# A feed-forward layer and its background tables: state-space table products moved from GpSimd to VectorE

## Chip, core and metric

The kernel runs on one core of a Trainium2 chip. The metric is device time in microseconds, from start to end of one execution. TensorE makes the matrix products, VectorE, ScalarE and GpSimd the elementwise work; SyncE's, ScalarE's and GpSimd's queues start the DMAs.

## What is computed

Eight layers over 512 tokens of 1024 features, in float32: a pooling mixer, a feed-forward layer with a convolution, windowed attention, a second feed-forward layer, an S5 state-space mixer, an MLP, a Mamba-2 mixer and an MLP. The change touches only what S5 needs ahead of time, out of its parameters alone. Cut to that, the reference says

```python
lam_bar = jnp.exp(lam * dt)
b_bar = ((lam_bar - 1) / lam)[..., None] * lax.complex(b_re, b_im)
bu = jnp.einsum('btgh,gph->btgp', u_blk, b_bar)
_, hs = lax.associative_scan(_s5_combine, (a_elems, bu), axis=1)
y = jnp.einsum('btgp,ghp->btgh', hs, c_mat).real
```

with 64 groups of 64 complex states and 16 channels. The kernel takes the tokens in 64 chunks of 8. Inside a chunk everything is products with small matrices: the powers of lam_bar from 0 to 8 (`pr`, `pi`), times B and C. From chunk to chunk the state is turned by a unit phasor and scaled. The tables that this needs (per group: the turns of 64 chunks, the matrices `vp` turned, `c4` and the products `kt`) are written to memory as `d_tab` and `d_k`, and the second feed-forward layer's background and S5 read them later.

## The kernel before

**Tables as background.** `s5_tables` (L535) is a generator: each `yield` ends a step, and other layers call for so many steps (`bg[0](n)`, `work(n)`) between their own work. Its first step is all of `s5_powers` (L558): exponentials and sines on VectorE and ScalarE, then powers one after the other and the repeated squares `step` by complex products on GpSimd (`cmul`, L617 to L623, each six instructions of 128x64). Then come eight rounds of four steps. `s5_phasors` (L645) makes the turns of eight groups by six doublings on GpSimd (L657 to L663, 8 to 256 elements wide), 36 instructions and a scaling, and starts two DMAs to `d_tab` from GpSimd's queue. `s5_mats` (L667) makes the matrices: one step of small VectorE work (L701 to L713: C turned and signed, `b0` and `b1`, of which `b1` has one buffer), then two halves of six 128x512 products each on GpSimd (L725 to L730). After the second half's products the first half's matrices are stored: `s5_store` (L737) transposes `vp` (L748) and multiplies (L749) on TensorE, copies out on ScalarE (L744, L751, L753), adds on VectorE (L757) and starts DMAs from ScalarE's queue. There are 34 steps.

**The layer around it.** Step 1 is taken in the pooling mixer (L916), the others in the body of the first feed-forward layer, `ffn_layer(0, ...)` at L1943. The head makes output tiles 0 and 1. The body (L980) has three phases, tiles 0 to 8, 8 to 16 and 16 to 22. In each phase pairs of tiles are made by products "upward" (96 of 512 columns for a pair: two tiles, gate and value, 8 k tiles, three products each), with four PSUM banks for the four outputs (`psm`, all four in use); VectorE takes them out (`scaled`, L936), convolves (L942, L943) and multiplies (L950), and ScalarE and VectorE part the result into `hi` and `lo` (L326, L328). After the first two phases `project` makes the eight outputs "downward" and `down` (L969) sums them. The third phase's downward products are the tail, made by halves of the tokens behind the body. A pair is followed by 3 steps of the tables, a downward output by 1, and 3 stand ahead of the first pair. `late` makes the rotary table of attention (`rope_tables`, L1024) ahead of the last phase. What is left of the tables is run at the body's end (`end_tables`, L1925). The second feed-forward layer is the same code with other work in its steps: it streams the conditioning's weights, with its sums on VectorE, ScalarE and TensorE (`ada_units`).

**Weights.** SyncE's queue loads chunks of 512 KB into three staging tiles; ScalarE (L204) and VectorE (L205) part each into `wh` and `wl`, of which there are four; a chunk serves 24 products.

**Order and room.** The tile framework fixes each engine's order of instructions when the program is built, by priority (the order of the program, seams raised) on a simulated time line; on the chip every engine runs its list in order. Tiles are slots of pools: `ap` has 31 of 128x512 and holds `hi`, `lo`, the eight outputs `ft`, the tables' `s5v` (2) and `s5buf` (6), the rotary table (2) and, in the last phase, 8 tiles of tail weights; `tp` has 14 for what lives shortly. An instruction that writes a tile waits until the last user of the slot's earlier tile is done.

Of the kernel before, what the change touches and what calls it, by code (L numbers as in the profile page):

```python
# [21 lines left out]
P = 128  # L22
# [7 lines left out]
# order of queueing: how many tiles each stage of a chain over the tiles stays behind the first, the tiles whose part  # L30
# falls to GpSimd, and the projections' steps between the blocks of attention and the chunks of SSD
# [32 lines left out]
def net_kernel(ctx: ExitStack, tc: tile.TileContext, I: dict, out: bass.AP, parts=ALL):  # L64
# [33 lines left out]
    # ---- constants  # L98
# [18 lines left out]
    r = 0  # L117
# [43 lines left out]
    # ---- x, feature-major  # L161
# [48 lines left out]
    def chunks(W, k0, nk, c0, ncol=256, kmax=4, gain=None, **kw):  # L210
        """(hi, lo, first k, k tiles) for the rows of k tiles k0.. and columns c0.. of W."""
        for k in range(0, nk, kmax):
            n = min(kmax, nk - k)
            r = (k0 + k) * P
            yield wchunk(W[r:r + n * P, c0:c0 + ncol].rearrange("(k p) n -> p k n", p=P),
                         gain=gain and (gain[0], gain[1] + k), **kw) + (k, n)
# [14 lines left out]
    def project(W, k0, nk, c0, tiles, xh, xl, evac, **kw):  # L231
        """Output tiles (an even run of them) over all tokens; evac(n, psum, span)."""
# [8 lines left out]
    class Held:  # L241
        """Output tiles taken over one half of the tokens, then over the other; their weights stay for both.
        runs: (W, k0, nk, c0, apart, kwargs) of one or two tiles each, which share a bank; the weights of the last
        `apart` k tiles lie among the activations."""
# [20 lines left out]
        def run(self, hf, xh, xl, evac):  # L265
            """evac(run, tile of the run, psum, span)"""
# [10 lines left out]
    # ---- root mean square over features (partitions and tiles)  # L277
    class Norm:
# [19 lines left out]
        def rs(self, span, eps, out=None):  # L298
            """1/rms of each token of the span, on all partitions."""
# [30 lines left out]
    class Line:  # L330
        """Keeps the instructions given to it in their order on their engine."""
# [11 lines left out]
    def staged(stages, lags):  # L343
        """Takes each k tile through the stages, every stage some tiles behind the first."""
# [13 lines left out]
    def warm_sqrt(after):  # L358
        """Has the square root's table loaded behind the given instruction, ahead of its use."""
# [4 lines left out]
    def behind(instructions):  # L364
        """Queues what it holds behind the given instructions on their engines."""
# [5 lines left out]
    class PreNorm:  # L371
        """The normalized, scaled (and shifted) x, in parts; one span at a time."""
# [40 lines left out]
    class PreScale(PreNorm):  # L413
        """x times the norm's gains alone, in parts; what the products give is then to be scaled by 1/rms."""
# [7 lines left out]
        def parts(self, span):  # L422
            """The two stages that make tile k's parts of the new x."""
# [14 lines left out]
    def post_add(ft, sq, gname, g0, span, nxt, pre):  # L438
        """x += rms_norm(f) over the span; nxt gathers the new squares."""
# [18 lines left out]
    def reduce_angle(a, k):  # L458
        """a less its nearest multiple of two pi; k is scratch."""
# [5 lines left out]
    def exp_exact(x, scr):  # L465
        """x to its exponential, to float32's accuracy; scr(dtype) gives scratch of x's shape."""
# [13 lines left out]
    # ---- a vector times a weight, laid out with features on partitions: in float32 by rows, summed over the  # L480
    # partitions as three bfloat16 parts, which hold all of its bits
    def vecmat(pool, W, ncb, col, done):
        """Steps, to be run between other work; done(cb, sums) takes the features of four tiles."""
# [35 lines left out]
    def ada_units(pool, i):  # L519
        """The modulation silu(c) @ W + b of layer i, and what S5's products make of its shift."""  # L520
# [14 lines left out]
    def s5_tables(pool, dr):  # L535
        """Chunk matrices of the state space, from its parameters alone; steps as of ada_units."""
# [3 lines left out]
        step = []  # L540
        s5_powers(pool, dr, pr, pi, cr, ci, sg, step)
# [5 lines left out]
        buf = [at("s5buf") for _ in range(6)]  # L547
        mats = s5_mats(pool, dr, pr, pi, vr, vi, cr, ci, sg, buf[3:])
        next(mats)
        for n in range(8):  # L550
            s5_phasors(dr, n, step, sg, buf)
            yield
            for _ in range(3):
                next(mats)
                yield
        yield from mats

    def s5_powers(pool, dr, pr, pi, cr, ci, sg, step):  # L558
# [58 lines left out]
        def cmul(orr, oi, ar, ai, br, bi, tmp):  # L617
            G.tensor_tensor(orr, ar, br, ALU.mult)
            G.tensor_tensor(tmp, ai, bi, ALU.mult)
            G.tensor_tensor(orr, orr, tmp, ALU.subtract)  # L620
            G.tensor_tensor(oi, ar, bi, ALU.mult)
            G.tensor_tensor(tmp, ai, br, ALU.mult)
            G.tensor_tensor(oi, oi, tmp, ALU.add)  # L623

        for t in range(2, 9):
            cmul(pr[:, t], pi[:, t], pr[:, t - 1], pi[:, t - 1], pr[:, 1], pi[:, 1], t1)
        # unit phasors of one chunk and its decay
# [3 lines left out]
        e1r, e1i = sm("e1r"), sm("e1i")  # L631
        V.tensor_scalar(e1r, cm, 1.0, None, ALU.add)
        V.tensor_copy(e1i, sn)
# [1404 lines left out]
```

## Time and profile before

| | us |
|---|---|
| runs of the kernel | 2565.32, 2565.53, 2560.61 |
| their median | 2565.32 |
| span of the profiled execution | 2564.4 |
| TensorE busy in it | 2368.0 (92%) |
| VectorE busy | 1687.6 (66%) |
| ScalarE busy | 1148.0 (45%) |
| GpSimd busy | 736.4 (29%) |

The time of the profiled execution itself is not listed apart from these runs; its span, from the first to the last instruction, is the number beside them. Busy shares are means over eight unlike layers, so a stage has to be read by its own stretch of the trace, and an engine with a small share can still be the one that a stage waits for. In the rows PE is TensorE's matmuls, DVE VectorE, ACT ScalarE, POOL GpSimd, SP SyncE; L205 is line 205 of the kernel.

### The profile page before, as it was taken

Reading aid. Unit: us, or ns where it says so; the run is one execution under the profiler, and the core shown is the slowest. Engines: PE = TensorE matmul, PEld = TensorE weight load, DVE = VectorE, ACT = ScalarE, POOL = GpSimd, SP = SyncE. Lnnn points to the kernel's source line nnn. Section 1 sums busy time; section 2 is a strip of 40 time slices with the busy share of each in tenths; the row PEclk is TensorE's granted clock in tenths of the full one; section 3 lists DMA queues with packets and bytes.
Section 4 is the critical chain, followed back from the end, with each engine's and each line's share of the span. In section 5 each row is a group of like instructions: output and inputs, shape, how many; then the busy total and the mean of one; then the engine's idle time right before and its main releaser. Section 6 shows DMA issues by size and latency. Waiting matters only on the chain.

```text
span 2564.4 us, 34249 instructions
## 1 busy us (share of the span) xinstructions
PE 2368.0 (92%) x12485; PEld 1989.4 (78%) x12485; DVE 1687.6 (66%) x2739; ACT 1148.0 (45%) x2054; POOL 736.4 (29%) x1111
## 2 busy tenths in 40 slices
PE   6888996998988999996989899999999999999998
PEld 6756674887677888776878787789887888888888
DVE  6874574667857868687653667665778788633333
ACT  6533342447666544343543433334556454423332
POOL 3989988031212000004120201112043332301110
PEclk8988997999999999998989999999999999999999
DMA  4234333222155555652852255553233332233322
GB/s 121 69 98 114 118 121 101 90 80 66 33 155 158 172 181 164 197 164 76 280 180 91 82 171 185 184 172 95 88 113 106 105 98 95 84 98 99 99 86 71
DMA packets 296761, 311.34 MB, mean 121 GB/s; under 512 B 53569, under 2 KB 251025, under 8 KB 295569
## 3 DMA queue, kind: packets, MB, share of 16 engines
q1 hardware_dynamic: 267729, 274.03, 35.2%
q10 hardware_dynamic: 23680, 17.31, 2.2%
q0 software_dynamic: 5184, 17.83, 2.1%
q8 instruction: 98, 1.61, 0.3%
q14 instruction: 70, 0.57, 0.1%
HBM read 284.92 MB, written 24.18 MB: 121 GB/s over the span
## 4 chain that ended last, share of the span: by engine, by line
PE 63%; DVE 12%; POOL 9%; DMA 6%; issue 5%; ACT 4%; SPq 0%; DVEq 0%; ACTq 0%; POOLq 0%
PE mm L220 18%; PE mm L219 18%; PE mm L221 18%; DVE wl L205 3%; DMA as<-in_ada_w 3%; POOL s5buf L659 1%; ACT wh L204 1%; PE pb L1710 1%; DVE u L400 1%; PE mm L1640 1%; PE mm L1641 1%; PE mm L1642 1%; DVE lo L328 1%; PE pn L306 1%; DVE u L450 1%
## 5 line engine op out<-in xcount | busy, mean ns | idle before, releaser
L220 PE MATMUL mm<-h,wh 128*128 128x512 f32 (+1 forms) x1792 | 669.4, 374 | 26.5 <-DVE h L428 13.2
L219 PE MATMUL mm<-h,wh 128*128 128x512 f32 (+1 forms) x1792 | 665.9, 374 | 27.2 <-ACT h L401 11.4
L221 PE MATMUL mm<-h,wl 128*128 128x512 f32 (+1 forms) x1792 | 666.3, 372 | 1.9 <-DVE wl L205 1.9
L205 DVE TENSOR_TENSOR wl<-ws,wh 128x1024 fp32r<-128x1024 f32 (+1 forms) x367 | 499.5, 1365 | 252.2 <-ACT wh L204 239.4
L204 ACT ACTIVATE wh<-ws 128x1024 fp32r<-128x1024 f32 (+1 forms) x367 | 387.2, 1059 | 531.0 <-PE mm L220 435.8
L220 PEld LDWEIGHTS mm<-h,wh 128*128 128x128 f32 x1792 | 348.1, 194 | 86.4 <-DVE h L428 16.9
L219 PEld LDWEIGHTS mm<-h,wh 128*128 128x128 f32 x1792 | 348.1, 195 | 84.1 <-ACT h L401 12.6
L219 PE MATMUL mm<-hi,wh 128*128 128x512 f32 (+1 forms) x1056 | 372.7, 357 | 27.4 <-ACT hi L326 22.3
L221 PEld LDWEIGHTS mm<-h,wl 128*128 128x128 f32 x1792 | 348.7, 195 | 56.8 <-DVE wl L205 2.3
L220 PE MATMUL mm<-lo,wh 128*128 128x512 f32 (+1 forms) x1056 | 373.4, 355 | 11.8 <-DVE lo L328 11.8
L221 PE MATMUL mm<-hi,wl 128*128 128x512 f32 (+1 forms) x1056 | 373.1, 355 | 0.0
L219 PEld LDWEIGHTS mm<-hi,wh 128*128 128x128 f32 x1056 | 201.1, 191 | 55.9 <-ACT hi L326 23.9
L1264 POOL TENSOR_TENSOR r<-r 128x512 f32<-128x512 f32 x64 | 88.0, 1379 | 517.3 <-ACT r L1260 384.2
L220 PEld LDWEIGHTS mm<-lo,wh 128*128 128x128 f32 x1056 | 202.1, 191 | 40.1 <-DVE lo L328 14.2
L221 PEld LDWEIGHTS mm<-hi,wl 128*128 128x128 f32 x1056 | 202.3, 192 | 26.5
L504 DVE SCALAR_TENSOR_TENSOR aa<-as,cond,aa 128x512 f32<-128x512 f32 x168 | 130.1, 774 | 112.8 <-DMA as<-in_ada_w 111.5
L296 POOL TENSOR_TENSOR acc<-acc,sq 128x256 f32<-128x256 f32 (+1 forms) x64 | 62.1, 972 | 389.6 <-ACT sq L295 377.7
L328 DVE TENSOR_TENSOR lo<-r,hi 128x512 fp32r<-128x512 f32 x64 | 48.1, 756 | 76.4 <-ACT hi L326 76.2
L1285 DVE SCALAR_TENSOR_TENSOR x<-mm,mod,x 128x512 f32<-128x512 f32 (+1 forms) x76 | 48.9, 662 | 60.3 <-PE mm L221 60.3
L512 ACT ACTIVATE ab<-aa 128x512 bf16<-128x512 f32 x72 | 45.0, 625 | 90.6 <-DVE aa L504 50.5
L1319 POOL DMA_DIRECT2D vt<-d_tab x16 | 8.8, 555 | 264.7 <-PE mm L221 260.8
L326 ACT ACTIVATE hi<-r 128x512 fp32r<-128x512 f32 x64 | 40.2, 630 | 70.4 <-POOL r L1264 70.3
(494 smaller groups left out, 4084.5 us busy)
## 6 DMA issues: line engine op xcount, KB each, us to landing
ws<-in_mlp_w SPq DMA_DIRECT2D x124, 512.0 KB, 3.9
as<-in_ada_w SPq DMA_DIRECT2D x192, 256.0 KB, 3.1
ws<-in_ffn_w_in SPq DMA_DIRECT2D x88, 512.0 KB, 4.2
ws<-in_m_w_in SPq DMA_DIRECT2D x41, 512.0 KB, 3.7
ws<-in_ffn_w_out SPq DMA_DIRECT2D x40, 512.0 KB, 4.7
ws<-in_w_o SPq DMA_DIRECT2D x16, 512.0 KB, 3.5
ct<-d_tab SPq DMA_DIRECT2D x8, 1024.0 KB, 5.9
ws<-in_s_w_glu SPq DMA_DIRECT2D x16, 512.0 KB, 5.8
```

The lines of the kernel that those rows point to most:

```text
L204: A.activation(h_, s_, AF.Copy)
L205: V.tensor_tensor(l_, s_, f(h_), ALU.subtract)
L219: T.matmul(ps, wh, xh, start=first, stop=False)
L220: T.matmul(ps, wh, xl, start=False, stop=False)
L221: return T.matmul(ps, wl, xh, start=False, stop=last).ins
L296: eng.tensor_tensor(dst, dst, sq[:, a:b], ALU.add)
L326: hi_ = A.activation(hi[:, ts], src, AF.Copy)
L328: return hi_, V.tensor_tensor(lo[:, ts], src, f(hi[:, ts]), ALU.subtract)
L504: V.scalar_tensor_tensor(acc, st, col(k), acc, ALU.mult, ALU.add)
L512: A.activation(parts[j], acc, AF.Copy)
L1264: G.tensor_tensor(r, r, r, ALU.mult)
L1285: V.scalar_tensor_tensor(xT[n][:, ts], ps, md(i, 5, n), xT[n][:, ts], ALU.mult, ALU.add)
```

## The change

The powers are made by doubling, three complex products of 64, 128 and 256 elements in place of seven of 64. The turns of a group's 64 chunks become an outer product of two tables of eight (`near`: turns 0 to 7, `far`: turns 0, 8, ... 56), six instructions of 512 elements for eight groups in place of 37 of 8 to 512. All of these products go from GpSimd to VectorE, and GpSimd keeps two memsets for each table of eight and `dd` in the store. The copy into `cp` goes to ScalarE. The turns' DMAs go from GpSimd's queue to SyncE's. `vp` and its scratch are tiles of their own in place of parts of `s5buf`. A half's products are two steps, and its matrices are stored after the next half's, so with one half waiting longer than before. There are 63 steps in place of 34, the powers being five of them, and the first feed-forward layer takes 4 at a time in place of 3, so that 61 are taken by the end of its body. The rotary table's frequencies are filled by 32 memsets in place of 128.

```diff
@@ s5_tables @@
     def s5_tables(pool, dr):
         pr, pi = (pool.tile([P, 9, 64], F32, name=nm("s5k")) for _ in range(2))
         cr, ci = (pool.tile([P, 64], F32, name=nm("s5k")) for _ in range(2))
         sg = pool.tile([P, 1], F32, name="s5sg")
-        step = []
-        s5_powers(pool, dr, pr, pi, cr, ci, sg, step)
+        far, near = ([at("s5ph").rearrange("p (g t) -> p g t", t=8) for _ in range(2)] for _ in range(2))
+        yield from s5_powers(pool, dr, pr, pi, cr, ci, sg, far, near)
         yield
         vr, vi = (at("s5v").rearrange("p (t g) -> p t g", t=8) for _ in range(2))
         for s in range(8):
             A.activation(vr[:, s], pr[:, 7 - s], AF.Copy)
             A.activation(vi[:, s], pi[:, 7 - s], AF.Copy, scale=sg)
-        buf = [at("s5buf") for _ in range(6)]
-        mats = s5_mats(pool, dr, pr, pi, vr, vi, cr, ci, sg, buf[3:])
+        mats = s5_mats(pool, dr, pr, pi, vr, vi, cr, ci, sg)
         next(mats)
         for n in range(8):
-            s5_phasors(dr, n, step, sg, buf)
-            yield
-            for _ in range(3):
+            yield from s5_phasors(dr, n, far, near)
+            for _ in range(5):
                 next(mats)
                 yield
         yield from mats
 
-    def s5_powers(pool, dr, pr, pi, cr, ci, sg, step):
+    def s5_powers(pool, dr, pr, pi, cr, ci, sg, far, near):
@@ s5_powers, s5_phasors @@
         def cmul(orr, oi, ar, ai, br, bi, tmp):
-            G.tensor_tensor(orr, ar, br, ALU.mult)
...
-        for t in range(2, 9):
-            cmul(pr[:, t], pi[:, t], pr[:, t - 1], pi[:, t - 1], pr[:, 1], pi[:, 1], t1)
+            V.tensor_tensor(orr, ar, br, ALU.mult)
...
+        yield
+        for w in (1, 2, 4):
+            o = slice(w + 1, 2 * w + 1)
+            top = [a[:, w].unsqueeze(1).broadcast_to([P, w, 64]) for a in (pr, pi)]
+            tmp = tt("cm")[:, :64 * w].rearrange("p (t g) -> p t g", t=w)
+            cmul(pr[:, o], pi[:, o], pr[:, 1:w + 1], pi[:, 1:w + 1], *top, tmp)
         r8 = dr["r8"]
         V.tensor_scalar(r8, ea, 8.0, None, ALU.mult)
         exp_exact(r8, scr())
-        e1r, e1i = sm("e1r"), sm("e1i")
-        V.tensor_scalar(e1r, cm, 1.0, None, ALU.add)
-        V.tensor_copy(e1i, sn)
-        e2r, e2i = sm("e2r"), sm("e2i")
+        yield
+        er_, ei_ = sm("e1r"), sm("e1i")
+        V.tensor_scalar(er_, cm, 1.0, None, ALU.add)
+        V.tensor_scalar(ei_, sn, sg, None, ALU.mult)
+        turn = er_, ei_
+        free = iter([(sm("e2r"), sm("e2i")), (lr, li), (dt, th), (er, nr), (ni, sc), (er_, ei_), (cm, sn), (ea, t1)])
+        def squared(z):
+            o, t = next(free), tt("cm")[:, :64]
+            V.tensor_tensor(o[0], z[0], z[0], ALU.mult)
+            V.tensor_tensor(t, z[1], z[1], ALU.mult)
+            V.tensor_tensor(o[0], o[0], t, ALU.subtract)
+            V.scalar_tensor_tensor(o[1], z[0], 2.0, z[1], ALU.mult, ALU.mult)
+            return o
         for _ in range(3):
-            cmul(e2r, e2i, e1r, e1i, e1r, e1i, t1)
-            e1r, e1i, e2r, e2i = e2r, e2i, e1r, e1i
-        free = [e2r, e2i, lr, li, dt, th, er, nr, ni, sc]
...
-    def s5_phasors(dr, n, step, sg, buf):
+            turn = squared(turn)
+        for tab in (near, far):
+            G.memset(tab[0][:, :, 0:1], 1.0)
+            G.memset(tab[1][:, :, 0:1], 0.0)
+            for w in (1, 2, 4):
+                by = [a.unsqueeze(2).broadcast_to([P, 64, w]) for a in turn]
+                tmp = tt("cm")[:, :64 * w].rearrange("p (g t) -> p g t", t=w)
+                lo, up = slice(0, w), slice(w, 2 * w)
+                cmul(tab[0][:, :, up], tab[1][:, :, up], tab[0][:, :, lo], tab[1][:, :, lo], *by, tmp)
+                if tab is near or w < 4:
+                    turn = squared(turn)
+            yield
+    def s5_phasors(dr, n, far, near):
         g8 = slice(8 * n, 8 * n + 8)
-        ct, si = (b.rearrange("p (g c) -> p g c", g=8) for b in buf[:2])
...
-        for j in range(6):
-            w = 1 << j
...
-        nc.gpsimd.dma_start(dr["tab"][n][:, :512], ct.rearrange("p g c -> p (g c)"))
-        nc.gpsimd.dma_start(dr["tab"][n][:, 512:1024], si.rearrange("p g c -> p (g c)"))
-    def s5_mats(pool, dr, pr, pi, vr, vi, cr, ci, sg, buf):
+        wide = lambda t: t.rearrange("p (g a b) -> p g a b", g=8, a=8)
+        fr, fi = (t[:, g8].unsqueeze(3).broadcast_to([P, 8, 8, 8]) for t in far)
+        nr_, ni_ = (t[:, g8].unsqueeze(2).broadcast_to([P, 8, 8, 8]) for t in near)
+        for i, (a, b, c, d, op) in enumerate(((fr, nr_, fi, ni_, ALU.subtract), (fr, ni_, fi, nr_, ALU.add))):
+            o, t = tt("ph"), tt("ph")
+            V.tensor_tensor(wide(o), a, b, ALU.mult)
+            V.tensor_tensor(wide(t), c, d, ALU.mult)
+            V.tensor_tensor(o, o, t, op)
+            nc.sync.dma_start(dr["tab"][n][:, 512 * i:512 * i + 512], o)
+            yield
+    def s5_mats(pool, dr, pr, pi, vr, vi, cr, ci, sg):
@@ s5_mats @@
             for hf in range(2):
                 g4 = slice(8 * gb + 4 * hf, 8 * gb + 4 * hf + 4)
                 o4 = slice(4 * hf, 4 * hf + 4)
-                vp, tc_ = (b.rearrange("p (g t h) -> p g t h", g=4, t=8) for b in (buf[1 + hf], buf[0]))
+                wide = lambda t: t.rearrange("p (g t h) -> p g t h", g=4, t=8)
                 cp = pool.tile([P, 4, 9, 16], F32, tag="cp", bufs=2, name=nm("cp"))
                 tp8 = lambda a: a.unsqueeze(2).broadcast_to([P, 4, 8, 16])
                 pw = lambda a: a[:, :, g4].rearrange("p t g -> p g t").unsqueeze(3).broadcast_to([P, 4, 8, 16])
-                G.tensor_copy(cp[:, :, 0], cc[:, 0, o4])
-                G.tensor_tensor(cp[:, :, 1:], tp8(cc[:, 0, o4]), pw(pr[:, 1:]), ALU.mult)
-                G.tensor_tensor(tc_, tp8(cc[:, 1, o4]), pw(pi[:, 1:]), ALU.mult)
-                G.tensor_tensor(cp[:, :, 1:], cp[:, :, 1:], tc_, ALU.add)
-                G.tensor_tensor(vp, tp8(b0[:, o4]), pw(vr), ALU.mult)
-                G.tensor_tensor(tc_, tp8(b1[:, o4]), pw(vi), ALU.mult)
-                G.tensor_tensor(vp, vp, tc_, ALU.add)
-                if pend:
-                    s5_store(pool, dr, *pend.pop())
+                t = wide(tt("ct"))
+                A.activation(cp[:, :, 0], cc[:, 0, o4], AF.Copy)
+                V.tensor_tensor(cp[:, :, 1:], tp8(cc[:, 0, o4]), pw(pr[:, 1:]), ALU.mult)
+                V.tensor_tensor(t, tp8(cc[:, 1, o4]), pw(pi[:, 1:]), ALU.mult)
+                V.tensor_tensor(cp[:, :, 1:], cp[:, :, 1:], t, ALU.add)
+                yield
+                vp, t = wide(at("vp")), wide(tt("ct"))
+                V.tensor_tensor(vp, tp8(b0[:, o4]), pw(vr), ALU.mult)
+                V.tensor_tensor(t, tp8(b1[:, o4]), pw(vi), ALU.mult)
+                V.tensor_tensor(vp, vp, t, ALU.add)
                 pend.append((gb, hf, cp, vp, b0, dg))
                 yield
-        s5_store(pool, dr, *pend.pop())
+                if len(pend) > 1:
+                    s5_store(pool, dr, *pend.pop(0))
+        while pend:
+            s5_store(pool, dr, *pend.pop(0))
+            yield
@@ ffn_layer @@
-    def ffn_layer(l, phases, late=None):
+    def ffn_layer(l, phases, late=None, rate=3):
...
-            bg[0](3)
+            bg[0](rate)
...
-                    bg[0](3)
+                    bg[0](rate)
@@ rope_tables @@
         fr = tt("fr")[:1, :P]
         for i in range(32):
-            for r in range(4):
-                G.memset(fr[:, 32 * r + i:32 * r + i + 1], float(ROPE_FREQ[i]))
+            G.memset(fr.rearrange("o (r i) -> o r i", r=4)[:, :, i:i + 1], float(ROPE_FREQ[i]))
@@ net_kernel @@
             layer = ffn_layer(0, ((0, 8), (8, 16), (16, 22)),
-                              lambda: rope_c.update(rope_tables()) if "attn" in names else None)
+                              lambda: rope_c.update(rope_tables()) if "attn" in names else None, 4)
```

## Rows read from the trace of the kernel before

**Rows 1.** Page, 40 slices: busy tenths of POOL, TensorE's granted clock in tenths

```profile
POOL 3989988031212000004120201112043332301110
...
PEclk8988997999999999998989999999999999999999
```

**Rows 2.** Stretches: us, busy (instructions) of PE, PEld, DVE, ACT, POOL, clock, DMA

```profile
101.40:518.30 416.90, 361.01 (x1558) 277.34 (x1557) 271.35 (x326) 162.64 (x222) 317.21 (x624) 0.92 0.37 112
818.00:1131.00 313.00, 311.85 (x1479) 253.62 (x1477) 251.78 (x368) 140.09 (x185) 1.14 (x2) 1.00 0.55 169
...
818.00:892.00 74.00, 74.00 (x343) 60.99 (x341) 67.34 (x98) 42.35 (x55) 0.00 (x0) 1.00 0.53 164
...
450.00:518.30 68.30, 68.30 (x303) 56.27 (x302) 48.34 (x68) 32.04 (x40) 0.70 (x2) 1.00 0.33 101
```

**Rows 3.** TensorE's waits, 101.4 to 518.3: total us, times, longest

```profile
PE mm L219 <- ACT hi L326: 22.3, 3, 11.6
PE pb L748 <- POOL s5buf L730: 19.9, 5, 8.2
PE mm L220 <- DVE lo L328: 10.3, 1, 10.3
PE mm L219 <- DVE u L936: 3.3, 1, 3.3
```

**Rows 4.** VectorE's waits, same stretch

```profile
DVE b L711 <- POOL s5buf L729: 48.3, 6, 15.0
...
DVE lo L328 <- POOL s5buf L728: 12.8, 1, 12.8
```

**Rows 5.** Timeline, VectorE: start us, us, engine, line, operation, out<-in [idle before]

```profile
154.22 14.32 DVE L205 TENSOR_TENSOR wl<-ws,wh 128x1024 fp32r<-128x1024 f32 x1 [2.38 <-ACT wh L204]
...
259.47 11.29 DVE L205 TENSOR_TENSOR wl<-ws,wh 128x1024 fp32r<-128x1024 f32 x1 [3.24 <-ACT wh L204]
...
342.08 7.18 DVE L943 SCALAR_TENSOR_TENSOR tg<-u,vec,tg 128x510 f32<-128x510 f32 x1
...
403.89 12.11 DVE L328 TENSOR_TENSOR lo<-tv,hi 128x512 fp32r<-128x512 f32 x1 [12.84 <-POOL s5buf L728]
```

**Rows 6.** Timeline, GpSimd, beside the first of these

```profile
154.28 1.28 POOL L730 TENSOR_TENSOR s5buf<-s5buf,s5buf 128x512 f32<-128x512 f32 x1
...
167.49 1.60 POOL L663 TENSOR_SCALAR s5buf<-s5buf,s5sg 128x512 f32<-128x512 f32 x1
```

**Rows 7.** Timeline, TensorE: the first and last of 18 like products, and a store

```profile
142.25 0.39 PE L219 MATMUL mm<-h,wh 128*128 128x512 f32 x1
...
153.83 0.39 PE L219 MATMUL mm<-h,wh 128*128 128x512 f32 x1
...
231.60 0.27 PE L748 MATMUL pb<-ident,s5buf 128*128 128x128 f32 x1
...
233.87 0.50 PE L219 MATMUL mm<-hi,wh 128*128 128x512 f32 x1
```

**Rows 8.** Timeline, VectorE, second feed-forward layer

```profile
852.10 0.68 DVE L950 TENSOR_TENSOR tv<-tv,tg 128x512 f32<-128x512 f32 x1
852.70 1.21 DVE L205 TENSOR_TENSOR wl<-ws,wh 128x1024 fp32r<-128x1024 f32 x1
853.84 0.68 DVE L514 TENSOR_TENSOR aa<-aa,ab 128x512 f32<-128x512 f32 x1
```

**Rows 9.** Timeline, VectorE, ahead of the body

```profile
69.36 0.21 DVE L610 TENSOR_TENSOR s5k<-s5k,sc 128x64 f32<-128x64 f32 x1
69.49 0.21 DVE L612 TENSOR_TENSOR t<-nr,lamT 128x64 f32<-128x64 f32 x1
...
69.96 0.28 DVE L708 TENSOR_TENSOR b<-bs,s5k 128x128 f32<-128x128 f32 x1
70.16 0.28 DVE L711 TENSOR_TENSOR b<-bs,s5k 128x128 f32<-128x128 f32 x1
```

**Rows 10.** Page, DMA issues: out<-in, queue, count, KB each, us to landing

```profile
ws<-in_ffn_w_in SPq DMA_DIRECT2D x88, 512.0 KB, 4.2
```

More of the change, by code (lines that the diff above doesn't have):

```diff
@@ L617, in cmul @@
         def cmul(orr, oi, ar, ai, br, bi, tmp):
-            G.tensor_tensor(orr, ar, br, ALU.mult)
[L619 to L623, printed above, removed]
-        for t in range(2, 9):
-            cmul(pr[:, t], pi[:, t], pr[:, t - 1], pi[:, t - 1], pr[:, 1], pi[:, 1], t1)
+            V.tensor_tensor(orr, ar, br, ALU.mult)
+            V.tensor_tensor(tmp, ai, bi, ALU.mult)
+            V.tensor_tensor(orr, orr, tmp, ALU.subtract)
+            V.tensor_tensor(oi, ar, bi, ALU.mult)
+            V.tensor_tensor(tmp, ai, br, ALU.mult)
+            V.tensor_tensor(oi, oi, tmp, ALU.add)
+        yield
[4 more added lines that the diff above has]
+            cmul(pr[:, o], pi[:, o], pr[:, 1:w + 1], pi[:, 1:w + 1], *top, tmp)
         r8 = dr["r8"]
@@ L630, in s5_powers @@
         exp_exact(r8, scr())
-        e1r, e1i = sm("e1r"), sm("e1i")
-        V.tensor_scalar(e1r, cm, 1.0, None, ALU.add)
-        V.tensor_copy(e1i, sn)
-        e2r, e2i = sm("e2r"), sm("e2i")
-        for _ in range(3):
-            cmul(e2r, e2i, e1r, e1i, e1r, e1i, t1)
-            e1r, e1i, e2r, e2i = e2r, e2i, e1r, e1i
-        free = [e2r, e2i, lr, li, dt, th, er, nr, ni, sc]
-        for j in range(6):
-            step.append((e1r, e1i))
-            if j < 5:
-                e1r, e1i = free[2 * j], free[2 * j + 1]
-                cmul(e1r, e1i, step[-1][0], step[-1][1], step[-1][0], step[-1][1], t1)
@@ L645, in s5_phasors @@
-    def s5_phasors(dr, n, step, sg, buf):
-        g8 = slice(8 * n, 8 * n + 8)
-        ct, si = (b.rearrange("p (g c) -> p g c", g=8) for b in buf[:2])
-        tm = buf[2][:, :256].rearrange("p (g c) -> p g c", g=8)
-        G.memset(ct[:, :, 0:1], 1.0)
-        G.memset(si[:, :, 0:1], 0.0)
-        for j in range(6):
-            w = 1 << j
-            sr = step[j][0][:, g8].unsqueeze(2).broadcast_to([P, 8, w])
-            sj = step[j][1][:, g8].unsqueeze(2).broadcast_to([P, 8, w])
-            a0, a1, t = slice(0, w), slice(w, 2 * w), tm[:, :, :w]
-            G.tensor_tensor(ct[:, :, a1], ct[:, :, a0], sr, ALU.mult)
-            G.tensor_tensor(t, si[:, :, a0], sj, ALU.mult)
-            G.tensor_tensor(ct[:, :, a1], ct[:, :, a1], t, ALU.subtract)
-            G.tensor_tensor(si[:, :, a1], ct[:, :, a0], sj, ALU.mult)
-            G.tensor_tensor(t, si[:, :, a0], sr, ALU.mult)
-            G.tensor_tensor(si[:, :, a1], si[:, :, a1], t, ALU.add)
-        G.tensor_scalar(si, si, sg, 0.0, ALU.mult, ALU.add)
-        nc.gpsimd.dma_start(dr["tab"][n][:, :512], ct.rearrange("p g c -> p (g c)"))
-        nc.gpsimd.dma_start(dr["tab"][n][:, 512:1024], si.rearrange("p g c -> p (g c)"))
```

## Prediction

> **What bounds the kernel now.** I read the page's forty slices first: GpSimd is busy 80 to 90% in slices 2 to 7, nothing in slice 8, and TensorE's granted clock drops to 0.8 and 0.7 of its full level in four of the first seven slices, and in two of the other 33 [rows 1]. That stretch is the tables' work beside the first feed-forward layer. [...] The second layer shows what the products cost when nobody is in the way.
>
> The waits of TensorE in the first layer add to 55.8 us: 19.9 for the transposes of vp, which wait on GpSimd itself; 22.3 for hi on ScalarE; 10.3 and 3.3 for VectorE [rows 3]. Behind ScalarE and VectorE stands GpSimd as well. VectorE waits 48.3 us before line 711, because b1 has one buffer and GpSimd has not yet read the last one, and 12.8 us before a lo [rows 4]; whatever stands behind these on its in-order queue is late too. That lo goes on behind GpSimd's last read of vr, which fits a shortage of tiles in the pool `ap`. And four VectorE instructions that elsewhere take about 1.2 or 0.7 us last 14.32, 11.29, 7.18 and 12.11 us [rows 5]. The first begins as GpSimd begins a run of two-input products and ends just after GpSimd comes to a one-input one [rows 6]. So GpSimd is the bound of this stretch by three ways: its results, its hold on b1 and the tiles, and its way of holding VectorE up.
>
> **The floor of the stretch.** Back-to-back products follow each other by 11.58 us for 51, so 0.227 us each; a store's eight small products take from 231.60 to 233.87, so 2.27 us [rows 7]. The layer has 20 tiles x 2 x 8 x 3 = 960 products upward and 8 x 8 x 3 x 2 = 384 downward: 1344 x 0.227 = 305. Sixteen stores add 36, the sixteen turns of cs and the rest some 2 (estimate): 344 us. So of 416.9 some 56 are waits and 17 the half-speed stretches after them. The second layer's 313.0, its conditioning's small sums included, agrees with 305.
>
> **The parts.**
> GpSimd loses nearly all of its 317 us; this was the bound, so the 56 + 17 = 73 us are what can be won.
>
> VectorE gains 8 x 6 products for the turns and 16 x 6 for the matrices, 144 of 512 elements. None of that shape with these broadcast operands stands in the trace. Plain ones start 0.60 us apart; 128 wide with a broadcast operand start 0.20 apart, against 0.13 for 64 plain [rows 8, 9], so the broadcast seems to cost nothing. I take 0.60: 86 us. The bounds are 0.60 and GpSimd's own 1.28 for such a product [rows 6]. [...]
>
> Powers and eight-step tables: three doublings of three widths, 6 instructions each, 18 x (0.13 + 0.20 + about 0.34 by interpolation) = 12 us, and 8 squarings of 4 at 0.13 = 4; the r8 exponential, moved into the body, some 2 [rows 9].
>
> Cover, stage by stage. The 57 later steps carry 86 us and about 16 of small work that is there already, 1.8 each. A pair of upward tiles is 96 x 0.227 = 21.8 us of TensorE, plus four steps' share of the stores, 2.7: 24.5. VectorE's own share of a pair is 48.34/3 = 16.1, from the stretch of three pairs behind the tables, the rotary table included [rows 2]; four steps add 7.2: 23.3, or 95%. In the second layer's first pairs VectorE is busy 67.34 of 74.00 and TensorE 74.00 at clock 1.00 [rows 2], so such a load is hidden, but barely. A downward pair has 12.2 us of TensorE against 1.14 x 2 + 0.60 x 2 + 2 x 1.8 = 7.1, so it catches up. If this cover goes, VectorE is what is late next.
>
> Three exposed remainders. (a) The body opens with four steps, about 20 us of VectorE in a lump, against 1.2 us of slack in each pair; four prepared weight chunks (4 x 24 x 0.227 = 22 us) stand before it. Bounds 0 and 20; I take 6. (b) Tiles of `ap`: 8 outputs, 16 hi and lo and now 7 or 8 of the tables (8 before) exceed 31, and the tables now last to the body's end, where 8 tiles of tail weights and 2 of the rotary table join. Bounds 0 and the 22 of before (11.6 + 10.3, which I lay to ScalarE behind GpSimd and to a tile); I take 6, since the release now waits for one VectorE step. (c) VectorE's in-order queue before evacuations: 0 to 45 (below); 4.
>
> No cost: the later store only gives the transposes a vp that is half a batch old; it leaves two stores behind the last pair, counted in the 36. The 16 table writes move from GpSimd's queue to SyncE's, where weight loads stand behind one that waits for a product: a step of 1.8 us at worst each time, 29 in all if uncovered, against three staged chunks of 5.4 us and a landing of 4.2 [rows 10]. Sixteen small copies go to ScalarE, busy 163 of 417 [rows 2]; 96 fewer one-element fills on GpSimd are off the path. Ahead of the body GpSimd's power chain leaves VectorE alone: 0 to 3 us won; taken as 0.
>
> **Sum.** Body 344 + 16 = 360 against 416.9: 57 us less. The span is 2564.4; the profiled execution's own time isn't listed apart, the runs' median, 2565.32, is 0.9 above it. 2564.4 + 0.9 - 57 = about 2508.
>
> **Rivals.**
> *VectorE becomes the bound.* In each of ten pairs the four steps (7.2 us) stand ahead of evacuations; a bank falls due every 12 products, 2.7 us, so TensorE waits up to 4.5. Ten times that, 45, and 6 for tiles: body 395, 2543. GpSimd's 1.28 for the 144 would do about the same: 98 us more, and VectorE 5.7 over TensorE in a pair. For it: 95%; against: the second layer's 91% without a wait.
> *Tiles of `ap` run out, and it is slower.* A lo waits for a vp, whose transposes stand on TensorE's queue behind the pair's products. Each such wait costs the 11 us of [rows 3]; if all seven pairs of the last two phases have one, 77 us: 2585. It turns slower from six. For it: the count above, and tables that now outlast the last phase; against: one short step frees a tile.
> *The long VectorE rows aren't GpSimd's doing.* Then they stay. They hold 44.9 us where about 3.5 belong. If a VectorE instruction loses at most one GpSimd instruction, 1.28 us, only 5 of the 41 go: 36 worse than forecast, 2544. [...] The trace speaks against so short a wait: 14.32 us span a whole run [rows 5, 6].
> *The change does nothing:* TensorE's waits only change their names, 2565.
>
> **Chances.** Forecast 0.65, VectorE bound 0.20, long rows stay 0.05, nothing 0.04, slower by tiles 0.06. A measurement tells 0.2%, 5 us. Faster is the first three, 0.90; same 0.04; slower 0.06. The range goes from 2490 (no remainder, 73 us, and up to 3 ahead of the body) to 2545, which takes in VectorE as the bound.
>
> **What would show it.** Right: the body about 360 us, clock near 1.00; no TensorE wait on GpSimd; no VectorE instruction above 2.5 us; line 711's wait gone; GpSimd under 15 us in the body; VectorE about 290 to 310. (a) shows as a wait in the first pair, (b) as hi or lo waiting late in a phase, (c) as TensorE waiting for u. Wrong: long VectorE rows without GpSimd; new products well above 0.60; or a body above 400.

## The result, and the profile after

The changed kernel takes 2523.84 us, the median of four runs (2522.2 to 2528.55), against 2563.69 us for the kernel before, four runs beside them; the ratio is 0.985, with a 95% interval of 0.9835 to 0.9863. The range of the prediction holds it; the likeliest time, 2508, was 15.8 us too low. The medians are 39.9 us apart. The spans of the two profiled executions, one run each, go from 2564.4 to 2520.5 us, by 43.9; the stretches below are of these two.

The page's slices of the changed kernel, beside [rows 1]: GpSimd is at 0 to 3 tenths where it was at 8 and 9, and one slice of the first seven (the third) still shows the clock at 0.8 of its full level.

```profile
POOL 2202131131321000014111210112133432301110
PEclk9989999989999999997999999999999999999999
```

The stretches of the changed kernel, with the columns of [rows 2]: the body, from the first to the last 512-column product; its opening, and the rest of it; then what follows up to attention's first score product, cut at the first product of the norm (line 306).

```profile
98.80:454.40 355.60, 341.44 (x1519) 267.71 (x1517) 295.10 (x547) 155.62 (x224) 51.72 (x45) 0.98 0.40 121
98.80:180.00 81.20, 67.04 (x284) 54.95 (x283) 77.73 (x188) 34.16 (x55) 0.00 (x0) 0.89 0.35 105
180.00:454.40 274.40, 274.40 (x1236) 212.76 (x1235) 217.37 (x361) 121.45 (x169) 51.72 (x45) 1.00 0.42 126
...
454.40:503.80 49.40, 44.94 (x325) 40.73 (x323) 29.60 (x57) 22.61 (x44) 11.64 (x14) 0.90 0.41 131
503.80:569.20 65.40, 52.97 (x315) 47.46 (x316) 46.46 (x99) 40.70 (x104) 21.90 (x24) 0.87 0.14 46
```

The same two stretches behind the body in the kernel before:

```profile
518.30:540.00 21.70, 21.57 (x178) 21.16 (x178) 11.19 (x21) 9.43 (x18) 2.21 (x3) 1.00 0.26 75
540.00:612.30 72.30, 63.63 (x428) 59.06 (x426) 51.81 (x117) 45.36 (x116) 24.45 (x28) 0.95 0.20 62
```

Read together they say where the time went. The body is 61.3 us shorter (416.9 to 355.6) and starts 2.6 us earlier: 63.9 gained by its end. The seam, from the body's end to the first score product, takes 114.8 us instead of 94.0: 20.8 are given back, and 43.1 are left. Everything after that moves the gain by 0.8 us only (43.9 at the end). So the body did what was forecast, a little better, and the shortfall lies in one place outside it.

TensorE's waits in the changed kernel from the body's start to the first score product, the longest four. Inside the body only the first is left of the 55.8 us in [rows 3]: nothing waits on GpSimd, on hi or on lo. The other three are in the seam.

```profile
PE mm L219 <- DVE u L952: 14.2, 1, 14.2
PE mm L220 <- DVE h L428: 5.0, 3, 2.5
PE mm L219 <- ACT wh L204: 4.1, 3, 2.3
PE mm L219 <- ACT h L427: 3.8, 2, 2.7
```

VectorE's lines in the body of the changed kernel, three of them: no instruction is above 1.6 us, and the new products last 0.68, with broadcast operands (means of 0.678 to 0.686 by line) or without (0.674 to 0.683). Its wait at line 711 [rows 4], now line 722, is gone.

```profile
L205 DVE TENSOR_TENSOR wl<-ws,wh 128x1024 fp32r<-128x1024 f32 x54 | 65.8, 1220 | 44.6 <-ACT wh L204 44.4
...
L672 DVE TENSOR_TENSOR ph<-s5ph,s5ph 128x512 f32<-128x512 f32 x16 | 10.9, 678 | 0.0
...
L738 DVE TENSOR_TENSOR ct<-cc,s5k 128x512 f32<-128x512 f32 x14 | 9.5, 681 | 0.0
```

Now the seam. ScalarE's timeline in the changed kernel, just behind the body: the parts of three chunks of attention's weights (line 195; one row stands) and the copies of the last two table stores (vt, kt, c) stand ahead of the first squares of the tail's output (line 292), at 500.25.

```profile
485.93 1.71 ACT L195 ACTIVATE wh<-ws,vec 128x256 fp32r<-128x256 f32 x4 [15.40 <-PE mm L220]
...
494.99 0.60 ACT L767 ACTIVATE vt<-pb 128x512 f32<-128x512 f32 x1 [3.02 <-PE pb L764]
...
496.99 0.65 ACT L767 ACTIVATE vt<-pb 128x512 f32<-128x512 f32 x1
...
500.25 0.71 ACT L292 ACTIVATE acc<-f 128x256 f32<-128x256 f32 x2
```

And VectorE's timeline beside it: the outputs f that these squares need are there from 474 on, and the last two vp are made at 486.9 to 491, 32 to 37 us behind the body's end.

```profile
474.05 0.75 DVE L992 TENSOR_TENSOR f<-f,mm 128x256 f32<-128x256 f32 x2 [3.70 <-PE mm L221]
...
486.88 1.29 DVE L742 TENSOR_TENSOR vp<-b,s5v 128x512 f32<-128x512 f32 x2
...
490.53 0.69 DVE L744 TENSOR_TENSOR vp<-vp,ct 128x512 f32<-128x512 f32 x1
```

In the kernel before, the first squares (ScalarE, line 292) came 0.45 us after the first f (VectorE, line 976):

```profile
529.03 0.76 DVE L976 TENSOR_TENSOR f<-f,mm 128x256 f32<-128x256 f32 x2 [2.75 <-PE mm L221]
```

```profile
529.48 0.75 ACT L292 ACTIVATE acc<-f 128x256 f32<-128x256 f32 x2 [2.46 <-DVE f L976]
```

So before had 178 of TensorE's instructions in the stretch up to the norm: the 144 products of the tail's first half, 33 of the second's and the norm's first. It kept the other 111 to run beside the norm's chain. After has 325 there: the 288 products of both halves, the three stores' 36 and the end of the body's last product. Nothing of the tail is left, and the chain stands bare. The 20.8 us are, by the stretches: three table stores that moved behind the body, 3 x 2.27 = 6.8 [rows 7]; 8.1 more of TensorE idle (114.8 - 97.9 busy, against 94.0 - 85.2); and the remaining 5.9 go with the granted clock, 0.90 and 0.87 against 1.00 and 0.95. Of the 8.1, only 3.8 lie behind the cut, beside the bare chain (65.4 - 53.0 against 72.3 - 63.6). The other 4.3 lie ahead of it, where TensorE waits 4.1 us for the tail's first weights. The longest of those waits, 2.3 us, is for a part that stands on ScalarE's queue behind a store's copies (ScalarE's rows, then TensorE's):

```profile
455.90 1.12 ACT L760 ACTIVATE c<-cp 128x512 f32<-128x512 f32 x1
...
457.83 1.04 ACT L204 ACTIVATE wh<-ws 128x1024 fp32r<-128x1024 f32 x1
```

```profile
458.92 0.58 PE L219 MATMUL mm<-hi,wh 128*128 128x256 f32 x1 [2.32 <-ACT wh L204]
```

### The profile page after: what moved, and what is told of

The parts are those of the page before. It is cut to its first block, busy times and chain, and to the rows that moved or that the text cites. A ratio compares the mean times of both kernels' runs of the same rounds, so it can differ in the third digit from the quotient of the medians.

```text
span 2520.5 us, 33869 instructions
## 1 busy us (share of the span) xinstructions
PE 2358.8 (94%) x12485; PEld 1986.4 (79%) x12485; DVE 1717.7 (68%) x2969; ACT 1151.8 (46%) x2070; POOL 454.9 (18%) x489
## 4 chain that ended last, share of the span: by engine, by line
PE 70%; DVE 12%; DMA 7%; ACT 5%; issue 4%; POOL 1%; SPq 0%; DVEq 0%; ACTq 0%; POOLq 0%
PE mm L220 20%; PE mm L219 20%; PE mm L221 20%; DMA as<-in_ada_w 4%; DVE wl L205 2%; DVE aa L504 1%; DMA tz<-d_k 1%; ACT wh L204 1%; PE pb L1725 1%; PE mm L1655 1%; DVE u L450 1%; PE mm L1656 1%; PE mm L1657 1%; PE pn L306 1%; PE pb L765 1%
## 5 line engine op out<-in xcount | busy, mean ns | idle before, releaser
L219 PE MATMUL mm<-h,wh 128*128 128x512 f32 (+1 forms) x1792 | 665.0, 374 | 40.5 <-DVE u L952 14.2
L205 DVE TENSOR_TENSOR wl<-ws,wh 128x1024 fp32r<-128x1024 f32 (+1 forms) x367 | 467.2, 1277 | 256.0 <-ACT wh L204 247.6
L771 POOL TENSOR_TENSOR dd<-ident,s5dg 16x64 f32<-16x64 f32 x16 | 56.6, 3539 | 327.5 <-DVE kt L773 320.3
```

The costliest lines, as they stand in the source:

```text
L205: V.tensor_tensor(l_, s_, f(h_), ALU.subtract)
L219: T.matmul(ps, wh, xh, start=first, stop=False)
L771: G.tensor_tensor(dd, ident[:16, :16].unsqueeze(1).broadcast_to([16, 4, 16]), dg[:, g4].unsqueeze(2).broadcast_to([16, 4, 16]), ALU.mult)
```

## The experiments

The twelve runs and the two kernels in one table, from their traces and times: start of the body, its length, the seam, the longest wait of TensorE for u in the body, and the median time.

```
                               start   body    seam   u      time
before                         101.4  416.9    94.0   3.3   2563.7
after                           98.8  355.6   114.8  14.2   2523.8
e1_two_steps_down               98.1  360.8    94.7  14.2   2536.3
e2_one_step_at_opening          98.7  358.9    94.1  10.5   2529.2
e3_products_on_gpsimd           98.6  369.6   116.9  14.3   2540.0
e4_store_step_earlier           98.4  354.6   114.9  14.2   2519.8
f1_two_steps_down_first_only    97.5  360.5    94.7  14.2   2510.2
f5_powers_on_gpsimd             99.0  356.4    93.9   7.5   2503.1
f7_finer_steps                  98.3  346.3    94.0   2.9   2495.0
f8_powers_in_pool_layer        123.8  344.3    94.8    -    2517.9
b1_before_rate_4               100.8  412.2    94.8    -    2563.7
m1_before_matrices_on_vector   102.0  385.2    95.3    -    2537.0
e6_turns_by_scalar_queue        98.6  354.9   113.8  14.2   2524.1
g1_finer_steps_early_store      99.6  350.0    93.8   4.4   2496.3
```

**Where do the seam's 20.8 us come from?** The steps add up to 63, and the loops take 61: 1 in the pool layer, 4 at the opening, 4 behind each of ten pairs, 1 behind each of sixteen downward tiles. The last four stand behind the last pair, so 57 are dealt out ahead of the body's end and six behind it: the products of the last two halves and the last three stores, and the trace shows nearly all of them there. The first run gives the tables more steps, in the downward phases.

```diff
-                        bg[0](1)
+                        bg[0](2)
```

> After, with two table steps instead of one behind each downward tile; the tables then end before the last phase. Theory (the tables' last three stores lie behind the body and with them the order of the seam to attention changes, which gives back 20.8 us): the stretch from the body's end to the first score product falls from 114.8 to about 94, the body grows by the three stores of 2.27, 6.8 us, to about 362; span 2520.5 - 20.8 + 6.8 = about 2507, time about 2510. Rival (VectorE's total load takes the gain, wherever the steps stand): the seam may shorten, but the downward pairs have 5 us of slack for 3.6 of further steps and whatever is gained comes back as waits on VectorE in the body; time about 2524 or above.

Body 360.8 and seam 94.7, both as the theory had them, and 15.7 us gained at the first score product (553.5 against 569.2). But the time is 2536.3, a miss. The edit was wider than meant: the line serves both feed-forward layers, and in the second it doubled the steps of the conditioning. There the first to the last u are 332.1 us apart instead of 300.4, with waits for the conditioning's small sums. So once more with the first layer alone:

```diff
-                        bg[0](1)
+                        bg[0](1 if l else 2)
```

> After, with two table steps behind each downward tile in the first feed-forward layer alone (the run with two steps down also doubled the steps of the conditioning in the second layer, whose body took 332 us there against 300). Theory (the seam's 20.8 us come from the tables' end, and the loss of that run was the second layer's doubled steps alone): body about 361, seam about 94.5, first score product at 553.5 as in that run, 15.7 us ahead of after, and nothing lost behind it: time about 2508. Rival (whatever the first layer gains is lost again by the second): about 2524 or above, with the second layer's body above 310 us.

Measured 2510.2, ratio to before 0.979 (0.977 to 0.9815). The stretches of this run, cut at the norm as above: 178 instructions ahead of it again.

```profile
458.00:480.00 22.00, 21.57 (x178) 21.17 (x177) 11.57 (x21) 9.51 (x19) 2.21 (x3) 1.00 0.23 74
480.00:552.70 72.70, 64.60 (x427) 59.99 (x426) 51.75 (x116) 45.31 (x116) 24.39 (x28) 0.93 0.20 62
```

It follows that the tables' end behind the body cost the 20.8 us, and that VectorE's load is not what takes the gain: it had 10 us more of work in this body (304.8 against 295.1) and the same single wait. That the order fixed at build time is what turned is read from the timelines; why the simulated time line behind it chose so was not tried.

Two other things could have made the seam: the later store itself, and SyncE's new writes ahead of the tail's weights. Undone one by one, the store's place first:

```diff
                 pend.append((gb, hf, cp, vp, b0, dg))
-                yield
                 if len(pend) > 1:
                     s5_store(pool, dr, *pend.pop(0))
+                yield
```

> After, with each store issued at the end of the step that makes the next vp, one step earlier, as in the kernel before. Theory (the later store costs and gains nothing): body 355 +/- 3, time within 5 us of 2524. Rival (the delay is what took away TensorE's wait for vp): the transposes wait on VectorE, up to 2 or 3 us at each of 16 stores, body 370 to 400, time 2540 to 2565.

2519.8: within the 5 us, with the same seam (114.9) and the same wait. The 4 us lie in the attention layer, which took 254 to 266 us from its first score product to the second layer's conditioning in these versions, for no cause looked for here.

```diff
-            nc.sync.dma_start(dr["tab"][n][:, 512 * i:512 * i + 512], o)
+            nc.scalar.dma_start(dr["tab"][n][:, 512 * i:512 * i + 512], o)
```

> After, with the 16 writes of the turns issued from ScalarE's queue instead of SyncE's. Theory (they cost nothing on SyncE's queue, as the prediction has it): time within 4 us of 2524, the same wait of 14.2 and the same seam. Rival (behind SyncE's writes the weights of the tail come late, which makes part of the 20.8 us): the wait for the tail's weights, 4.1 us, goes, the seam falls below 108, time 2516 or less.

2524.1, seam 113.8, and 3.4 us of the wait for the tail's weights remain: SyncE's queue cost nothing.

**The wait of 14.2 us.** Timelines of the changed kernel: on VectorE the small work of the powers begins at 103.17 and goes on past 132 (two rows of it stand here), and the first u comes at 134.1; TensorE stands until then.

```profile
103.17 0.21 DVE L619 TENSOR_TENSOR cm<-s5k 128x64 f32<-128x64 f32 x1
...
132.27 0.28 DVE L620 TENSOR_TENSOR s5ph<-s5ph,cm 128x128 f32<-128x128 f32 x1
```

```profile
120.42 0.39 PE L221 MATMUL mm<-h,wl 128*128 128x512 f32 x1
...
134.97 0.77 PE L219 MATMUL mm<-h,wh 128*128 128x512 f32 x1 [14.16 <-DVE u L952]
```

The first try took one step instead of four ahead of the body, besides the two steps down (again in both layers, so that its time says little).

```diff
-            bg[0](rate)
+            bg[0](1)
             for ph, (j0, j1) in enumerate(phases):
```

> As the run before it, and one table step instead of four ahead of the body. Theory (the 14.2 us wait of the first pair is the lump of powers that stands ahead of the first pair's u on VectorE's queue): with the lump spread behind the first pairs the wait mostly goes, body about 350, time about 10 below the run before it, some 2500. Rival (the lump only moves, since a pair has about 1.2 us of slack on VectorE): a wait of 10 to 14 us stands behind the second pair instead, time as the run before it, 2510.

Here the rival was right: body 358.9, and a wait of 10.5 us behind the second pair in place of the 14.2. The next three change the first layer alone. One keeps the two steps down and moves the small products to GpSimd, in all six lines of cmul:

```diff
-            V.tensor_tensor(orr, ar, br, ALU.mult)
+            G.tensor_tensor(orr, ar, br, ALU.mult)
...
```

> The run before it, with the complex products of the powers and of the two eight-step tables (54 small instructions) on GpSimd and the rest on VectorE. Theory (the 14.2 us wait in the first pair is the lump of this small work ahead of u on VectorE's queue): the wait falls to 5 us or less, body about 350, time about 2497. Rival (VectorE's turns then wait in order for GpSimd's tables, and the instructions of both engines stretch each other): TensorE waits as long or longer for u, time 2508 to 2520.

2503.1. The wait halves but does not go. TensorE's and VectorE's waits in this run show the rival's part: the turns wait for GpSimd's tables on VectorE's queue, and u behind them. No VectorE instruction was stretched above 1.8 us.

```profile
PE mm L219 <- DVE u L952: 8.8, 3, 7.5
```

```profile
DVE ph L672 <- POOL s5ph L620: 5.5, 1, 5.5
...
DVE ph L673 <- POOL s5ph L623: 1.4, 1, 1.4
```

One cuts the powers into finer steps, a yield behind each doubling, and gives them out where VectorE has room:

```diff
             cmul(pr[:, o], pi[:, o], pr[:, 1:w + 1], pi[:, 1:w + 1], *top, tmp)
+            yield
...
             turn = squared(turn)
+        yield
...
-            yield
+                yield
...
-            bg[0](rate)
+            bg[0](rate if l else 1)
...
-                    bg[0](rate)
+                    bg[0](rate if l or ph else 3)
...
-                        bg[0](1)
+                        bg[0](1 if l else 3)
```

> After, with the powers cut into finer steps (a step for each doubling), one step at the opening, three for each pair of the first phase and three behind each downward tile, in the first layer alone. Theory (the lump of the opening counts, and VectorE has room for it if spread to the downward pairs): waits on VectorE in the body below 5 us in sum instead of 14.2, body 348 to 352, seam about 94.5, time about 2497. Rival (the first phase has no room on VectorE at all, as the run with one step at the opening showed with its 10.5 us wait in the second pair): 10 us or more of waits stay, time about 2508.

2495.0, ratio to before 0.9725 (0.970 to 0.975): the best version, 29 us below the change. Its body and seam:

```profile
98.30:444.60 346.30, 343.40 (x1556) 269.11 (x1556) 305.06 (x565) 164.19 (x236) 50.05 (x51) 1.00 0.45 134
444.60:538.60 94.00, 84.87 (x603) 79.90 (x602) 63.35 (x137) 54.83 (x134) 26.63 (x31) 0.96 0.21 65
```

VectorE does as much there as in the run with two steps down (305 us), at full clock and with 2.9 us of waits. So the load is not the trouble; the lump and its place are. Finer steps and more of them behind the downward tiles came together here, so what each gave alone is not shown. The last of the three, again with two steps down, takes the powers in the pool layer:

```diff
-                    work(1)
+                    work(4)
                 banded(1)
```

> After with two steps behind each downward tile of the first layer, and four table steps instead of one taken in the pool layer, so that the powers come before the first feed-forward layer. Theory (VectorE is idle 8.5 us of the 41 before the body's start): the wait of the first pair goes, the body starts 5 to 10 us later than 98.8, time 2500 to 2505. Rival (the lump delays the pool layer's norm by all of its 20 us or more): the body starts at 115 or later, time 2510 to 2525.

2517.9, the rival's time, but not through the norm. Its body has no wait of TensorE at all, but it starts 25 us late, because TensorE waits for a load of vectors (the wait is the longest of the stretch from 40 to 124 us; the body's row stands first):

```profile
123.80:468.10 344.30, 344.30 (x1556) 268.95 (x1555) 286.06 (x467) 164.15 (x236) 63.70 (x51) 1.00 0.45 134
```

```profile
PE mm L145 <- DMA rt<-in_ffn_conv_w: 20.7, 2, 19.9
```

SyncE's queue issues the first of the vectors' loads at 70.8 us, against 41.1 in the changed kernel. Two weight loads stand ahead of it there, and the load itself waits 14.5 us for VectorE's small products of the two eight-step tables. So the lump still delays the layer, through a queue (SyncE's waits, 53 to 72 us):

```profile
SPq L191 <- DVE nr L595: 14.6, 1, 14.6
SPq L140 <- DVE s5ph L621: 14.5, 1, 14.5
```

The last run adds the earlier store (diff above) to the finer steps:

> The run with finer steps, with the store a step earlier as well. Theory (the store's place costs nothing once TensorE waits for nothing in the body): within 4 us of 2495. Rival (the 4 us that the earlier store gave alone are real and add): 2491 or less.

2496.3, ratio 0.973 (0.972 to 0.975): the 4 us of the earlier store alone do not add.

**Engine, amount or pace?** The kernel before with four steps instead of three in the first layer (and at the opening of the second, which the first line serves too):

```diff
-            bg[0](3)
+            bg[0](4)
...
-                    bg[0](3)
+                    bg[0](4 if l == 0 else 3)
```

> The kernel before, with four table steps instead of three at each place of the first feed-forward layer; nothing else of the change. Theory (GpSimd's 317 us of work are the bound, not how they are dealt out): the body stays at 405 to 430, long VectorE rows and waits on GpSimd remain, time within 15 us of 2564. Rival (the pace of the steps was a part of the gain): body below 400, time 2545 or less.

2563.7, ratio 0.9998 (0.9989 to 1.0007): pace alone is worth nothing. The changed kernel with its 144 products on GpSimd, in the nine lines of the turns and matrices:

```diff
-            V.tensor_tensor(wide(o), a, b, ALU.mult)
+            G.tensor_tensor(wide(o), a, b, ALU.mult)
...
-                V.tensor_tensor(vp, vp, t, ALU.add)
+                G.tensor_tensor(vp, vp, t, ALU.add)
```

> After, with the 144 table products of 512 elements given back to GpSimd; the outer product, the doubling and the later store stay. Theory (the engine counts: GpSimd's two-input products hold VectorE up and its results come late): GpSimd is busy some 144 x 1.28 = 184 us and more in the body, VectorE instructions of over 2.5 us are back, the body is 375 to 400, time 2540 to 2565. Rival (the smaller number of instructions alone made the gain, since 184 us of GpSimd is no bound in a body of 355): time 2524 or less, as VectorE is relieved of 86 us.

2540.0, at the lower edge of the theory, with a body a little shorter than it said: 369.6, so 47 of the 61 us are there already with GpSimd doing fewer instructions, 210 us of work instead of 317. The engine of these products is worth the other 14, and the long VectorE rows are back. Which part of the rest gave the 47 (the fewer and wider products, the powers on VectorE or something smaller) was not separated. The row of the body; then VectorE's longest, a product of 64 elements that lasts 0.20 elsewhere; then the first and the last of the eleven GpSimd products that run beside it, each of 512 elements with two inputs:

```profile
98.60:468.20 369.60, 344.92 (x1519) 267.98 (x1517) 307.14 (x407) 153.02 (x219) 210.05 (x181) 0.97 0.39 115
```

```profile
199.35 11.89 DVE L773 TENSOR_TENSOR kt<-kt,dd 16x64 f32<-16x64 f32 x1 [0.31 <-ACT kt L769]
```

```profile
199.16 1.28 POOL L739 TENSOR_TENSOR cp<-cp,ct 128x512 f32<-128x512 f32 x1
...
210.10 1.06 POOL L673 TENSOR_TENSOR ph<-s5ph,s5ph 128x512 f32<-128x512 f32 x1
```

And the kernel before with the matrices alone on VectorE, in their six lines:

```diff
-                G.tensor_tensor(cp[:, :, 1:], tp8(cc[:, 0, o4]), pw(pr[:, 1:]), ALU.mult)
+                V.tensor_tensor(cp[:, :, 1:], tp8(cc[:, 0, o4]), pw(pr[:, 1:]), ALU.mult)
...
-                G.tensor_tensor(vp, vp, tc_, ALU.add)
+                V.tensor_tensor(vp, vp, tc_, ALU.add)
```

> The kernel before, with the 96 products of the matrices on VectorE; turns by doubling and powers stay on GpSimd. Theory (what counts is how long GpSimd still works with two inputs: 317 less some 114 us stay, about 200, as in the run with the products on GpSimd, whose body took 369.6): body 365 to 395, seam 94 as before, long VectorE rows remain, time 2515 to 2545. Rival (the matrices were the whole of it, since TensorE waits for vp alone): body 361 or less, time 2508 or less.

2537.0 and a body of 385.2, as the theory said, but not by its way: no VectorE instruction is above 1.75 us. GpSimd is busy 253 us, not 200, and VectorE now waits for GpSimd's smallest product, dd, which stands in GpSimd's queue among the turns. The body's row; then VectorE's longest wait, and TensorE's for a vp that comes late behind it:

```profile
102.00:487.20 385.20, 351.92 (x1554) 273.35 (x1555) 279.37 (x421) 163.16 (x222) 253.04 (x527) 0.95 0.40 120
```

```profile
DVE kt L757 <- POOL dd L755: 57.8, 7, 21.7
```

```profile
PE pb L748 <- DVE s5buf L730: 26.3, 2, 14.1
```

## Why the prediction was right, and where it was not

**The floor, 344 us, was right.** Where nothing stands in the way, TensorE is busy 343.4 us in the body with finer steps and 344.3 in the one with the powers ahead, both at clock 1.00. The half-speed stretches, to which the prediction laid 17 us, are in the trace of the kernel before: from 169.2 to 172.6, behind a wait of 3.34 us for u, the granted clock is 0.54 and the products start 0.43 us apart, against 0.227 ahead of it. TensorE's 361.0 busy us in that body [rows 2] are 17 above the floor.

**GpSimd as the bound: right.** Its three ways to hold the body up went with its work: no wait for it is left in the body, none at the old line 711, and no long VectorE row. The long rows came back with the products on GpSimd, which settles the rival that had them from elsewhere.

**VectorE's price and cover: right.** Taken at 0.60 us each, the products follow each other so:

```profile
456.32 0.69 DVE L738 TENSOR_TENSOR ct<-cc,s5k 128x512 f32<-128x512 f32 x1
456.93 0.69 DVE L743 TENSOR_TENSOR ct<-b,s5v 128x512 f32<-128x512 f32 x1
457.53 0.69 DVE L738 TENSOR_TENSOR ct<-cc,s5k 128x512 f32<-128x512 f32 x1
```

VectorE was forecast busy 290 to 310 us in the body and is 295.1; from 180 us on it hides the steps wholly (TensorE 274.40 of 274.40). A row lasts 0.69, but the next one starts 0.60 or 0.61 behind it: it is the 0.60 that each product adds to VectorE's time here.

**The remainders: right in sum, wrong in parts, and that is luck.** 16 were allowed. (a) was 14.2 us and not 6: the lump of powers stood ahead of u as a whole. (b) was 0 and not 6: no hi or lo waits in the body, so the count of tiles in `ap`, and the rival that ended slower, came to nothing. (c) was 0 and not 4. The body, 355.6, with the three stores that left it is 362.4, against a forecast of 360. The floor and the one wait make 358.2 of it. The other 4 were priced at nothing: they go with the opening's granted clock, 0.89, where 284 of TensorE's instructions take 67.0 us and would take 63 at the rest's pace (estimate, 274.40/1236 each).

**The step that failed** stands under "No cost": the later store "leaves two stores behind the last pair, counted in the 36". What lay behind the body was three stores and the last two vp, with their place in every engine's order. I priced two stores at 2.27 us each of TensorE, and never asked what is late next: the tail's first weights, one part of which stands on ScalarE's queue behind a store, and the norm of the tail's first half, whose chain had been covered by the second half's products. It cost 20.8 us: 6.8 are the stores, 4.3 the idle time ahead of the norm, 3.8 that beside its bare chain, and 5.9 go with the granted clock. Without it the sum holds: with the tables ended in time the kernel takes 2510.2, against the 2508 forecast. The later store as such, blamed in that sentence, was free, and so were SyncE's writes, as said.

**GpSimd under 15 us in the body: wrong**, at no cost, since nothing in the body waits for GpSimd. It shows 51.7, nearly all from dd, 13 products of 64 elements (below).

**Ahead of the body** 0 was taken of 0 to 3; it was 2.6.

The chance for the forecast, 0.65, stood for the right mechanism. The rival with VectorE as the bound holds for one pair only, the first.

## What to carry to other kernels

Work that is dealt out in steps beside a loop has an end, and the end has to be counted: steps needed against steps taken, and what stands just behind the last place where they are taken. Two steps left over, with the four dealt out behind the last pair, cost 14 us net here: the next stage's covering work was spent early, and its first weights came late. And where an engine is nearly full (VectorE 77.7 of 81.2 us in the opening here, with the first u behind the lump, at 134.1), look at the size and place of the largest lump, not at the load alone: the same 305 us of VectorE work cost 14.2 us of waits in coarse steps, and 2.9 in fine ones dealt out where the slack was.

## What the runs showed of the hardware that was not expected

In these traces VectorE and GpSimd hold each other up in both directions, for whole runs of instructions, fourteen and eleven in the two longest rows below. GpSimd's dd, a product of 64 elements, takes 0.283 us (median) in the kernel before and 3.786 in the one after, where VectorE runs two-input products without a gap. The rows of dd, before and after, and its longest, which spans fourteen VectorE instructions:

```profile
L755 POOL TENSOR_TENSOR dd<-ident,s5dg x16: 282/283/729, 19.2 to 424.4; 16x64 f32<-16x64 f32 x16
```

```profile
L771 POOL TENSOR_TENSOR dd<-ident,s5dg x16: 282/3786/8555, 18.8 to 496.5; 16x64 f32<-16x64 f32 x16
...
188.42 8.55 POOL L771 TENSOR_TENSOR dd<-ident,s5dg 16x64 f32<-16x64 f32 x1 [98.33 <-DVE kt L773]
```

So either engine, with a run going, kept the other's next two-input instruction back here: a dd lasted up to 8.55 us, a kt up to 11.89. Twelve of the sixteen dd in the changed kernel take over 0.9 us: ten end 0.15 to 0.16 us after a VectorE run, where VectorE stands idle for 0.03 us or more, and two end 0.22 us after the start of a VectorE instruction with an input from PSUM. The other way round, the kt of 11.89 us ends 0.08 us after its run of GpSimd products, but the row of 7.18 us [rows 5] ends while GpSimd's products go on, so a break is not always needed. A loss of one GpSimd instruction, 1.28 us, as the rival on the long rows has it, is less than what was measured: the rows of what was kept back span a run of eleven products (11.89 us) and one of fourteen instructions (8.55 us).
